# Weight sums in 32 spread pieces, and 512-column block products in the gated feed-forward

## The chip, the cores and the metric

One core of one Trainium2 chip runs the whole kernel. The metric is device time in microseconds (us), measured over the whole execution. The engines are named as the profile names them: PE (TensorE, the matrix multiplier), with PEld for its weight loads, DVE (VectorE), ACT (ScalarE), POOL (GpSimd) and SP (SyncE, which here only issues transfers). Sixteen DMA engines move data between HBM and on-chip memory, and also from HBM to HBM.

## The reference, cut to what matters

Two layers of an encoder work on 512 tokens of width 1024, all in float32. Each layer adds three things to the residual x: a mixer (neighbourhood attention, "NA", and grouped-query attention, "GQA", side by side), a cross attention to 256 memory tokens, and a gated feed-forward part with a short convolution. Only the last is computed differently by the change:

```python
def conv_ffn(h, w_up, conv_w, conv_b, w_down):
    u = h @ w_up                                   # 512 x 1024 times 1024 x 5632
    up = jnp.pad(u, ((0, 0), (1, 1), (0, 0)))
    u = up[:, :-2] * conv_w[0] + up[:, 1:-1] * conv_w[1] + up[:, 2:] * conv_w[2] + conv_b
    gate, val = jnp.split(u, 2, axis=-1)           # 2816 columns each
    return (jax.nn.silu(gate) * val) @ w_down
```

## The kernel before, in words

**Precision.** A matrix product in float32 is made of three reduced ones. Every operand is kept as a rounded part ("hi") and the rest ("lo"), and `mm3` (line 902) adds hi·hi, hi·lo and lo·hi in one PSUM bank. A weight tile is loaded by SP into one of three `raw` buffers, ACT rounds it to `hi` (line 784), POOL or DVE subtracts to get `lo` (line 785). Up to four such pairs exist; `get_w` prepares two tiles ahead of the one in use.

**Feed-forward units.** The 5632 columns of w_up are taken as 22 units j: 128 gate columns and the matching 128 value columns, for all 512 tokens. Units 0 to 5 (`PLAIN = 6`) are plain products: two sides, eight slices of the inner dimension, three matmuls of 512 token columns each, 48 in all. Units 6 to 21 use a block scheme with seven products in place of eight. Inner dimension, gate/value and token halves are each cut in two; with sums and differences of weight blocks and of token blocks, seven products of half the inner dimension and half the tokens (4 slices, three matmuls of 256 columns, so 84 matmuls) give both sides of the unit. `up_forms` (line 1922) does this in three PSUM banks, a, b and c, which it reads out with ACT copies and DVE additions between the products and after them. Then `convolve` applies the taps, the gate and the split of the result. From unit 6 on, rows of the down projection (six or five units times three matmuls of 512 columns for each of 8 rows and group) stand between the units.

**Weight sums.** The block scheme needs, for each layer, two matrices made out of w_up: `dr_sums` and `dr_diffs`, in HBM. `make_form` (line 704) makes one half of one of them in one call: a copy from HBM to HBM issued by ACT (the "base copy"), and then an accumulating transfer issued by POOL (line 714) on top of it. Each covers 16 units, 512 rows of 2048 columns, 4 MB. It is called in the first four steps of the neighbourhood attention of each layer (`na_quanta`, line 1683). One accumulating transfer reads another half, so it waits for that to be done.

**What sets the order.** The kernel is traced by loops that weave attention steps with filler products. SP issues its transfers in the order of this trace. For PE, ACT, DVE and POOL a planner (`Order`, line 348) reads the trace, gives each instruction a cost and a due time (the `Step.times` and `FAR_` numbers), and fixes an order by engine; there is no reordering when the kernel runs. An instruction that waits holds up everything behind it on its engine.

**Token operands.** Units 0 to 2 use unscaled tokens and multiply the PSUM result by the norm (`up_finish`). From unit 3 (`SCALED`) the tokens are scaled first (`scale_tokens`), split into hi and lo (`split_tokens`), and their block sums are made one by one (`token_forms`).

## Time and profile before

| | |
|---|---|
| median of 3 runs | 1416.34 us (1416.06 to 1418.67) |
| the profiled execution: its own time, and its span | 1416.2 us, 1414.3 us |
| PE busy | 1324.3 us, 94% of the span |
| DVE, ACT, POOL busy | 60%, 56%, 51% |
| mean granted TensorE clock | 0.969 of full |
| DMA | 229.78 MB, mean 162 GB/s |

The span runs from the first to the last instruction, and the execution's own time is 1.9 us longer. The stages of layer 0 lie at about 0 to 198 us (neighbourhood attention and its projections), 198 to 265 (grouped-query attention), 265 to 350 (memory attention) and 350 to 745 (feed-forward); layer 1 has the same stages at about 745 to 1400. In a table of windows each row gives, for a stretch, the busy time of each engine with its instruction count, the mean granted clock (PEclk, 1.00 is full), the busy share of the DMA engines and the rate in GB/s. Work of PE that is lost in a stretch is its idle time and, where the clock is below 1.00, that share of the busy time.

### The profile page before, as it was taken

How to read it: one execution, taken by the hardware profiler on the slowest of the kernel's cores; microseconds unless marked ns; L12 is line 12 of the kernel's file. 1: busy time of each engine (PE TensorE's matmuls, PEld its weight loads, DVE VectorE, ACT ScalarE, POOL GpSimd, SP SyncE). 2: the span in 40 equal slices, each digit the busy share in tenths (PEclk: the TensorE clock that was granted, in tenths of full speed). 3: DMA queues.
4: the chain of work that ended last, by engine and by line, in shares of the span. 5: the costliest groups of instructions: out<-in, count | busy, mean ns of one | idle time of the engine just before them, and what ended most of it. 6: DMA issues, size and time to landing. Idle time of an engine off the chain costs nothing.

```text
span 1414.3 us, 20974 instructions
## 1 busy us (share of the span) xinstructions
PE 1324.3 (94%) x7595; PEld 1158.5 (82%) x7595; DVE 843.6 (60%) x1729; ACT 788.1 (56%) x1459; POOL 721.3 (51%) x526
## 2 busy tenths in 40 slices
PE   9775899989999999999997759999899999999998
PEld 8664788868879999999886558888788899999997
DVE  6243787747596655555542538877576856554554
ACT  7244687646565555555542537875564555555544
POOL 2343696562645444444643337956453654444443
PEclk9887999999999999999998889999999999999999
DMA  7999958641324565555458998377322255555552
GB/s 237 307 305 247 222 142 179 141 134 42 113 85 127 147 171 145 149 144 150 120 163 296 325 262 201 107 178 161 107 68 82 86 168 149 162 150 145 150 154 75
DMA packets 262087, 229.78 MB, mean 162 GB/s; under 512 B 6880, under 2 KB 242912, under 8 KB 253792
## 3 DMA queue, kind: packets, MB, share of 16 engines
q1 hardware_dynamic: 253120, 160.94, 39.1%
q0 software_dynamic: 4224, 33.55, 11.6%
q10 hardware_dynamic: 4640, 33.95, 6.9%
q8 instruction: 60, 0.98, 0.3%
q14 instruction: 43, 0.35, 0.1%
HBM read 218.45 MB, written 69.21 MB: 203 GB/s over the span
## 4 chain that ended last, share of the span: by engine, by line
PE 78%; DMA 12%; DVE 3%; POOL 2%; ACT 2%; issue 1%; SPq 0%; POOLq 0%; ACTq 0%
PE mm L102 52%; PE sc L102 19%; PE tr L102 4%; DMA raw<-in_w_in 4%; DMA raw<-in_w_mem_q 3%; DMA t<-in_memT 2%; PE tr L1563 2%; POOL lo L785 1%; DMA dr_sums<-in_w_up 1%; DMA dr_diffs<-in_w_up 1%; DMA r<-in_bias 1%; PE tr L1408 1%; PE tr L1754 0%; ACT hi L784 0%; DVE t L1863 0%
## 5 line engine op out<-in xcount | busy, mean ns | idle before, releaser
L785 POOL TENSOR_TENSOR lo<-raw,hi 128x512 fp32r<-128x512 f32 (+3 forms) x293 | 521.4, 1789 | 538.3 <-ACT hi L784 486.7
L784 ACT CAST hi<-raw 128x512 fp32r<-128x512 f32 (+3 forms) x361 | 288.2, 812 | 269.3 <-DMA raw<-in_w_in 68.9
L102 PE MATMUL mm<-r,hi 128*128 128x512 f32 (+1 forms) x1344 | 387.5, 369 | 5.7 <-DVE xg L1008 5.7
L102 PE MATMUL mm<-xg,hi 128*128 128x512 f32 (+1 forms) x960 | 271.1, 368 | 3.2 <-ACT xg L1006 2.2
L102 PEld LDWEIGHTS mm<-r,hi 128*128 128x128 f32 x1344 | 238.6, 190 | 41.5 <-DVE xg L1008 6.1
L102 PE MATMUL mm<-r,lo 128*128 128x512 f32 (+1 forms) x704 | 251.3, 359 | 0.0
L102 PEld LDWEIGHTS mm<-xg,hi 128*128 128x128 f32 x960 | 173.0, 192 | 32.0 <-ACT xg L1006 2.6
L102 PE MATMUL mm<-xg,lo 128*128 128x512 f32 (+1 forms) x480 | 175.4, 365 | 0.0
L102 PE MATMUL sc<-r,hi 128*128 128x256 f32 (+1 forms) x832 | 163.9, 292 | 0.0
L102 PEld LDWEIGHTS mm<-r,lo 128*128 128x128 f32 x704 | 133.2, 189 | 20.2
L102 PEld LDWEIGHTS sc<-r,hi 128*128 128x128 f32 x832 | 133.7, 191 | 4.8
L102 PE MATMUL mm<-hi,xg 128*128 128x512 f32 (+1 forms) x384 | 117.9, 378 | 19.1 <-ACT t L1467 16.0
L102 PE MATMUL sc<-r,lo 128*128 128x256 f32 (+1 forms) x416 | 121.3, 291 | 0.0
L102 PEld LDWEIGHTS mm<-xg,lo 128*128 128x128 f32 x480 | 92.0, 192 | 14.6
L102 PEld LDWEIGHTS mm<-hi,xg 128*128 128x128 f32 x384 | 72.3, 201 | 30.2 <-ACT t L1467 16.3
L102 PE MATMUL sc<-r,r 128*128 128x256 f32 (+1 forms) x352 | 76.7, 340 | 18.4 <-ACT t L1386 18.4
L1063 POOL TENSOR_SCALAR t<-t,s 128x512 f32<-128x512 f32 (+1 forms) x112 | 67.0, 618 | 45.7 <-DVE s L1547 26.8
L102 PEld LDWEIGHTS sc<-r,lo 128*128 128x128 f32 x416 | 79.6, 191 | 1.2
L1950 DVE TENSOR_TENSOR tr<-mm,t 128x256 f32<-128x256 f32 x32 | 13.9, 433 | 111.5 <-PE mm L102 111.5
L785 DVE TENSOR_TENSOR lo<-raw,hi 128x1024 fp32r<-128x1024 f32 (+1 forms) x68 | 66.5, 978 | 20.2 <-ACT hi L784 20.1
L102 PEld LDWEIGHTS sc<-r,r 128*128 128x128 f32 x352 | 55.0, 197 | 25.7 <-ACT t L1386 19.8
L1863 DVE SCALAR_TENSOR_TENSOR t<-sc,minus,t 128x504 f32<-128x504 f32 (+1 forms) x128 | 56.1, 478 | 31.4 <-ACT t L1856 30.7
(210 smaller groups left out, 2296.1 us busy)
## 6 DMA issues: line engine op xcount, KB each, us to landing
raw<-in_w_up SPq DMA_DIRECT2D x56, 512.0 KB, 3.8
dr_sums<-in_w_up ACTq DMA_DIRECT2D x4, 4096.0 KB, 24.0
dr_diffs<-in_w_up ACTq DMA_DIRECT2D x4, 4096.0 KB, 19.3
raw<-dr_sums SPq DMA_DIRECT2D x32, 512.0 KB, 4.6
raw<-dr_diffs SPq DMA_DIRECT2D x32, 512.0 KB, 3.9
raw<-in_w_in SPq DMA_DIRECT2D x25, 512.0 KB, 5.4
raw<-in_w_down SPq DMA_DIRECT2D x32, 384.0 KB, 3.4
dr_sums<-in_w_up POOLq DMA_DIRECT2D x2, 4096.0 KB, 26.8
```

What stands on the lines that cost most here:

```text
L102: return self.engine.matmul(out, lhsT, rhs, **k)
L784: act.copy(hi[:, k], raw[:, k])
L785: (POOL if eng[0] == "P" else DVE).tensor_sub(lo[:, k], raw[:, k], f(hi)[:, k])
L1063: eng.tensor_scalar(e, e, sums[:, col : col + 1], 1.0, op0=ALU.mult, op1=ALU.mult)
L1408: PE.transpose(tr[:, (2 * i + c) * P : (2 * i + c + 1) * P], es[j][:, i, c * P : (c + 1) * P], ident)
L1563: PE.transpose(tr[:, k * P : (k + 1) * P], es[j][:, k * P : (k + 1) * P], ident)
L1863: DVE.scalar_tensor_tensor(cc[:, dst], u[:, src], wi, cc[:, dst], op0=ALU.mult, op1=ALU.add)
L1950: DVE.tensor_add(b[:, halves[1]], second, u2)
```

## The change

- `PLAIN` becomes 4: units 4 and 5 are block products too. `SCALED` is gone: units 0 to 3 all use unscaled tokens.
- The weight sums are made for four groups of units, (4, 4), (8, 4), (12, 5), (17, 5) as first unit and count. With two layers and four halves each that is 32 pieces, each a base copy of 512 rows by 512 or 640 columns (1 or 1.25 MB) and an accumulating transfer of the same size. The base copy is now issued by SP.
- The pieces wait in a list. One is taken at every third step of the grouped-query attention (six a layer), at four steps of the memory attention, and at every even unit of the feed-forward, in this order until the list is empty: layer 0 takes 10 before its feed-forward and 11 in it, and five of those already belong to layer 1.
- A token block holds its rounded part and the rest side by side, 256 columns each. A product is now, for each slice, one matmul of 512 columns (rounded weights times both) and one of 256 (the weights' rest times the rounded tokens): 56 matmuls a unit in place of 84. Since hi·hi and hi·lo then stand in two halves of a bank, each readout adds the halves: seven ACT copies, seven DVE and three POOL additions of 256 columns a unit, where there were three ACT copies and three DVE additions.
- All three blocks of tokens are split after unit 1, the sums are made after unit 2 and split after unit 3.
- The planner counts POOL's transfers as far (16 us, 1.3 us of POOL), and the base copies as ordinary ones.

The core of the diff (the new names are explained above; what is left out renames and moves):

```diff
-PLAIN = 6
-SCALED = 3
+PLAIN = 4
+SHARES_OF_FORMS = [(4, 4), (8, 4), (12, 5), (17, 5)]
...
-FAR_NS, FAR_POOL = 45000.0, 1500.0
+FAR_NS, FAR_POOL = 16000.0, 1300.0
...
+    form_queue = [(l, g, n) for l in range(DEPTH) for g in range(len(SHARES_OF_FORMS)) for n in range(4)]
...
+        l, g, n = form_queue.pop(0)
+        j, nj = SHARES_OF_FORMS[g]
...
-        act.dma_start(dst, base)
-        nc.gpsimd.dma_start(dst, more, accum_op=ALU.add, max_dma_last_dim=4 * 2048)
+        SP.dma_start(dst, base)
+        nc.gpsimd.dma_start(dst, more, accum_op=ALU.add, max_dma_last_dim=4 * P * nj)
...
         def na_quanta(s):
-            if s < 4:
-                make_form(l, s, ACT_IN_ORDER)
...
+        def gqa_quanta(s):
+            if s % 3 == 0:
+                make_form()
+            return [GQA_SLOT[s]]
...
+        def mem_quanta(s):
+            if s in (0, 2, 4, 6):
+                make_form()
+            return [MEM_FILL[s]]
...
+        def token_blocks():
             for name, k, n in (("b11", 0, 0), ("b21", 1, 0), ("b22", 1, 1)):
-                xform[name] = [v[:, 4 * k : 4 * k + 4, halves[n]] for v in (ffn.hi, ffn.lo)]
+                xform[name] = [rtile((2, S)) for _ in range(2)]
+                for v, src in zip(xform[name], quarter(k, n)):
+                    ACT.copy(v[:, :, halves[0]], src)
+                    DVE.tensor_sub(v[:, :, halves[1]], src, f(v)[:, :, halves[0]])
...
         def up_forms(j):
-            a, b, c = ps_s(), ps_t(), ps_mm()
+            a, b, c = ps_mm(), ps_t(), ps_s()
...
-                    mm3(ps, wh[:, i], wl[:, i], hi[:, k], lo[:, k], start and k == 0, k == 3, skip_group_check=not start)
+                    both = xform[form][k // 2][:, k % 2]
+                    PE.matmul(bank, wh[:, i], both, start=start and k == 0, stop=False, skip_group_check=True)
+                    PE.matmul(bank[:, halves[0]], wl[:, i], both[:, halves[0]], start=False, stop=k == 3, skip_group_check=True)
...
+            product(a, "gate", 0, "b11")
+            ACT.copy(p1, al)
+            DVE.tensor_add(p1, ah, p1)
+            product(b, "gate", 1, "b21")
+            ACT.copy(gb, bl)
+            POOL.tensor_add(gb, gb, p1)
+            DVE.tensor_add(bh, bh, gb)
+            product(c, "sums", 0, "t1")
+            ACT.copy(p5, cl)
+            DVE.tensor_add(p5, ch, p5)
+            product(a, "sums", 1, "t2", False)
+            ACT.copy(u2, al)
+            DVE.tensor_add(u2, ah, u2)
+            product(c, "diffs", 0, "b22", False)
+            ACT.copy(vc, cl)
+            POOL.tensor_add(vc, vc, u2)
+            DVE.tensor_add(bl, ch, vc)
+            product(a, "diffs", 1, "t3", False)
+            ACT.copy(va, al)
+            POOL.tensor_add(va, va, p5)
+            DVE.tensor_add(cl, ah, va)
+            product(a, "val", 0, "t4", False)
+            ACT.copy(l4, al)
+            DVE.tensor_add(ch, ah, l4)
+            convolve(j, [b, c])
...
+            if n % 2 == 0:
+                make_form()
             if n == 0:
                 up_first()
                 scale_tokens()
+                token_blocks()
             elif n > 1:
                 up(n)
+                if n == PLAIN - 2:
+                    token_sums()
+                elif n == PLAIN - 1:
+                    split_sums()
```

The planner and the loops move instructions, which the diff does not show. Three moves follow; in a row stand the line of the kernel, the operation, the tile written, the tiles read and the shape (partitions by columns); "x2" is two such instructions in a row.

First, the base copies. ACT in the neighbourhood attention of layer 0, before: `dr_sums` is one matrix of weight sums, `hi` rounded weights.

```order
L784 CAST hi_393<-raw_312 128x512 x2
L1059 ACTIVATE r_401<-mm_405,s_328 128x4x64 x2
L79 DMA dr_sums_78<-in_w_up 512x2048
L784 CAST hi_520<-raw_391 128x512 x2
L784 CAST hi_591<-raw_399 128x512
L1059 ACTIVATE r_402<-mm_458,s_328 128x4x64
L784 CAST hi_591<-raw_399 128x512
L79 DMA dr_sums_78<-in_w_up 512x2048
L1059 ACTIVATE r_402<-mm_458,s_328 128x4x64
```

Two base copies of 4 MB stand among its work; with the change ACT issues none. SP in the grouped-query attention of layer 0, with the change (`raw` are loads of weights):

```order
L79 DMA raw_1700<-in_w_out 128x4x256
L79 DMA dr_sums_78<-in_w_up 512x512
L79 DMA raw_1777<-in_w_out 128x4x256
L79 DMA raw_1842<-in_w_mem_kv 128x8x128
L79 DMA dr_sums_78<-in_w_up 512x512
L79 DMA raw_1899<-in_w_mem_kv 128x8x128
L79 DMA raw_2001<-in_w_out 64x4x256 x2
L79 DMA dr_diffs_79<-in_w_up 512x512
```

Base copies now stand between the weight loads of SP's own queue, one to every one to three loads. Second, SP in the feed-forward of layer 0, with the change (`in_w_up 128x4x128` are the value weights of a unit):

```order
L79 DMA raw_4390<-dr_sums_80 128x8x128
L79 DMA raw_4418<-dr_diffs_81 128x8x128
L79 DMA raw_4452<-in_w_up 128x4x128
L79 DMA dr_diffs_85<-in_w_up 512x640
L79 DMA raw_4486<-in_w_down 128x6x128
L79 DMA raw_4513<-in_w_up 128x8x128
```

Where the load of the down weights (`in_w_down`) came straight after that of the value weights, a base copy of 1.25 MB now goes ahead of it. Third, ACT in a block unit, before (`t<-sc` and `t<-mm` are the readouts, L1856 and L1865 the convolution and the gate):

```order
L1942 COPY t_4710<-sc_4707 128x256
L1056 CAST r_4678<-tr_4546 128x512
L784 CAST hi_4776<-raw_4716 128x768
L1946 COPY t_4711<-mm_4709 128x256
L1948 COPY t_4710<-sc_4707 128x256
L784 CAST hi_4808<-raw_4748 128x1024
L1856 ACTIVATE t_4826<-tr_4708,par 128x512
L784 CAST hi_4844<-raw_4780 128x1024
```

and with the change (L1961 to L1982 are the readouts, L789 the rounding of weights, L1870 the convolution, L1879 the gate):

```order
L1961 COPY t_4625<-mm_4622 128x256
L1968 COPY t_4626<-sc_4624 128x256
L1964 COPY t_4625<-tr_4623 128x256
L1879 ACTIVATE tr_4476<-t_4579 128x512
L789 CAST hi_4710<-raw_4660 128x1024
L1971 COPY t_4627<-mm_4622 128x256
L1062 CAST r_4593<-tr_4476 128x512
L1974 COPY t_4627<-sc_4624 128x256
L789 CAST hi_4744<-raw_4686 128x1024
```

Seven copies of banks stand where three stood, and the roundings of weights, each of which waits for a load, stand between them.

104 lines of the change are left out of this document (40 added, 64 removed).

## The prediction

> **What bounds the kernel now.** I first read the engines' shares at the head of the page (the span, 1414.3 us, stands in the table above), and then a table of windows, stage by stage.
>
> ```profile
> PE 1324.3 (94%) x7595; PEld 1158.5 (82%) x7595; DVE 843.6 (60%) x1729; ACT 788.1 (56%) x1459; POOL 721.3 (51%) x526
> ```
>
> ```profile
> core 0: us, PE busy (x) PEld busy (x) DVE busy (x) ACT busy (x) POOL busy (x), PEclk, DMA share, GB/s
> 50.00:125.00 75.00, 42.74 (x177) 33.72 (x176) 20.66 (x56) 26.53 (x70) 23.64 (x27) 0.77 0.95 304
> 125.00:175.00 50.00, 46.06 (x244) 38.74 (x244) 33.07 (x95) 32.39 (x86) 30.67 (x35) 0.93 0.94 220
> 175.00:275.00 100.00, 99.79 (x525) 82.92 (x525) 79.62 (x166) 74.00 (x159) 74.32 (x75) 1.00 0.62 150
> 275.00:300.00 25.00, 19.33 (x82) 15.63 (x81) 14.51 (x24) 12.09 (x20) 13.62 (x8) 0.93 0.79 185
> ...
> 425.00:675.00 250.00, 250.00 (x1728) 233.85 (x1727) 141.07 (x266) 135.93 (x200) 119.59 (x58) 1.00 0.52 147
> 750.00:800.00 50.00, 29.65 (x127) 24.01 (x126) 14.44 (x40) 16.83 (x45) 11.18 (x13) 0.80 0.97 314
> ...
> 825.00:875.00 50.00, 35.04 (x186) 29.78 (x184) 28.20 (x72) 23.87 (x61) 24.13 (x29) 0.83 0.97 228
> 875.00:975.00 100.00, 99.94 (x530) 83.27 (x529) 81.30 (x169) 77.04 (x162) 75.44 (x77) 1.00 0.59 144
> 975.00:1025.00 50.00, 45.99 (x222) 37.93 (x222) 29.44 (x63) 26.01 (x52) 26.61 (x16) 0.97 0.55 141
> ```
>
> Two regimes show. From 425 to 675 (and from 175 to 275, and 875 to 975) PE is busy all the time at full clock: PE is the bound, and only fewer or shorter matmuls help. In the other rows PE loses time while the DMA engines are busy at 0.8 to 0.97. Lost work is idle time plus the clock's share of the busy time. 50 to 125: 32.3 + 0.23 x 42.7 = 42.1. 125 to 175: 3.9 + 3.2 = 7.2. 750 to 800: 20.4 + 5.9 = 26.3. 825 to 875: 15.0 + 6.0 = 20.9. These four, all in neighbourhood attention, are **96.5 us**. The entries to the memory attention, 275 to 300 (5.7 + 1.4) and 975 to 1025 (4.0 + 1.4), add **12.4 us**.
>
> Who fills the DMA engines there? The chain of waits, the timeline of the issuing queues and the waits of SP:
>
> ```profile
> 40.02 25.89 DMA raw<-in_w_in
> 86.62 30.87 DMA t<-in_memT
> ...
> 269.50 20.65 DMA raw<-in_w_mem_q
> ...
> 822.37 21.90 DMA raw<-in_w_in
> ```
>
> ```profile
> 38.10 0.59 ACTq L79 DMA_DIRECT2D dr_sums<-in_w_up  x1
> 91.40 0.50 ACTq L79 DMA_DIRECT2D dr_diffs<-in_w_up  x1
> ```
>
> ```profile
> 264.27 1.03 POOL L714 DMA_DIRECT2D dr_diffs<-dr_sums  x1
> ```
>
> ```profile
> SPq L79 <- DMA dr_sums<-in_w_up: 52.3, 4, 13.6
> ```
>
> Ordinary loads of 0.25 to 0.5 MB take 16 to 31 us in the stretches in which the 4 MB base copies (first issue 38.1, last 91.4) and the last accumulating transfer (264.3) run. SP even stands 52 us behind base copies before it may issue its next load. So the lost 109 us are paid for the weight sums.
>
> **The change, part by part.**
>
> *Block products on PE.* Merged rows of the chain in the feed-forward, and from 400 to 436:
>
> ```profile
> 405.89 30.17 PE mm L102 x132
> 437.50 1.44 PE tr L102 x12
> ...
> 451.69 1.44 PE tr L102 x12
> ```
>
> A 512-column matmul takes 30.17 / 132 = 0.2286 us, a 256-column one 1.44 / 12 = 0.120. A block unit had 84 x 0.120 = 10.08 us and gets 28 x (0.2286 + 0.120) = 9.76, so 0.32 less; 16 units and two layers give 10.2. Units 4 and 5 had 48 x 0.2286 = 10.97 and get 9.76; four such units give 4.8. Together **-15.0 us**, straight on the bound. The rest of a unit's period (451.69 - 437.50 = 14.19) is 18 down matmuls, unchanged.
>
> The Trainium skill ("TensorE: Matmul & The Clock Gate", section "Back-to-back issue gap") speaks against most of this: it gives a warm gap of N/2.4 + 2.5 ns, 109 and 216 ns here, by which (an estimate) a unit would go only from 9.17 to 9.10 us and the sum would be 7.4 in place of 15.0. The rows above, with 120 and 229 ns, disagree with it; they decide.
>
> *Base copies out of the neighbourhood attention.* Nothing of the weight sums is left in it; of the 22.8 MB moved from 50 to 125 (75 x 304) most were the four base copies of 4.2 MB. Bounds: all 96.5 comes back, or, if other loads take the place, nothing. The row nearest to the state after is 175 to 275: the same attention loop at a DMA share of 0.62, with an accumulating transfer in it (rows of 214 to 240 below), loses 0.2 of 100. I take 85%, **-82 us**; the rest stays for bias and memory loads and for SP's copies within the chip, which are all in this stage.
>
> *Where the transfers go.* Part 3 of the page prices them:
>
> ```profile
> q0 software_dynamic: 4224, 33.55, 11.6%
> q10 hardware_dynamic: 4640, 33.95, 6.9%
> ```
>
> (0.116 + 0.069) x 1414.3 = 262 us of all 16 engines, so 8.2 for each of the 32 new pieces if smaller rows cost no more: 3.1 base copy, 5.1 accumulation. Six come in the 67 us of grouped-query attention, which without its accumulation needs some 16 us of DMA: 65 of 67, almost full. What a load suffers beside an accumulation, and what a unit can bear, by the transfers' issue to landing from 214 to 240 and from 440 to 700, and by rows of the timeline on the gate weights of one unit (and one more subtraction, on DVE):
>
> ```profile
> dr_sums<-dr_sums POOLq DMA_DIRECT2D x1, 4096.0 KB, 25.9
> raw<-in_w_mem_kv SPq DMA_DIRECT2D x2, 512.0 KB, 11.5
> ```
>
> ```profile
> raw<-in_w_up SPq DMA_DIRECT2D x14, 512.0 KB, 4.4
> ```
>
> ```profile
> 479.44 0.37 SPq L79 DMA_DIRECT2D raw<-in_w_up  x1
> 484.72 1.05 ACT L784 CAST hi<-raw 128x1024 fp32r<-128x1024 f32 x1
> 485.85 2.41 POOL L785 TENSOR_TENSOR lo<-raw,hi 128x1024 fp32r<-128x1024 f32 x1 [1.60 <-ACT hi L784]
> 488.46 1.21 DVE L785 TENSOR_TENSOR lo<-raw,hi 128x1024 fp32r<-128x1024 f32 x1
> 492.70 0.40 PE L102 MATMUL sc<-xg,hi 128*128 128x256 f32 x2
> ```
>
> 11.5 us were borne in grouped-query attention without loss, since weights are loaded long ahead: 0 for its 12 pieces. In the feed-forward a load is rounded 484.72 - 479.44 = 5.3 us after its issue and lands after 4.4, so it may be 0.9 late; then ACT, in order, stands, and behind the rounding stand its readouts of PSUM, on which the next products wait. A base copy ahead delays a load by up to 3.1 us, an accumulation beside it by up to 5.1. Bounds per piece: 0 (both fall between loads, or the weights' lead on PE covers it: 492.70 less 485.85 + 2.41 is 4.4 us) and 5.1 - 0.9 = 4.2. The planner knows the base copies, so I take 1.0 for the 12 pieces there: **+12** (0 to 50). For the memory attention's eight pieces 0.5 each, **+4** (0 to 14, by the 12.4 us that 8 MB cost at its entries). Of these 12.4 I expect half back, since smaller accumulations of the last steps still run there: **-6** (0 to -12.4). POOL's 32 issues of 1.03 us are 16 a layer, between work that fills half of it: 0.
>
> *Readouts.* A unit gains four ACT copies, four DVE additions and three POOL additions:
>
> ```profile
> 483.01 0.37 ACT L1946 COPY t<-mm 128x256 f32<-128x256 f32 x1 [0.68 <-PE mm L102]
> 485.95 0.43 DVE L1950 TENSOR_TENSOR tr<-mm,t 128x256 f32<-128x256 f32 x1 [3.51 <-PE mm L102]
> ```
>
> ```profile
> 143.22 0.72 POOL L1473 TENSOR_TENSOR t<-t,t 128x256 f32<-128x256 f32 x1
> ```
>
> ACT +1.5, DVE +1.7, POOL +2.2 us. From 425 to 675 a unit of 14.19 us holds 7.7, 8.0 and 6.8 of them; now 9.2, 9.7 and 9.0 of about 13.87, up to 70%. From 175 to 275 they are at 74 to 80% with PE full, so the amount is covered. The order is tighter: the second product in bank c comes one product (28 / 7 = 4 slices, 1.39 us) after the first, and in between ACT must copy and DVE add, 0.68 to start, 0.37 and 0.43, 1.48 with nothing in the way. The same holds between the second and third product in bank a. Down rows or the next unit's products fill such gaps where the planner can. Units 4 and 5 have no down rows. I take 0.2 for each of 36 units, **+7** (0 to 40).
>
> Splitting tokens earlier moves the same work; its cover is units 1 to 3, about 33 us of PE, and DVE is the engine that could be late: **+1** (0 to 6).
>
> **Sum**, against the profiled execution's own 1416.2 (span 1414.3, 1.9 around it; the median is 1416.34, so nothing is to be converted): 1416.2 - 15.0 - 82 - 6 + 12 + 4 + 7 + 1 = 1337.2. Forecast **1337 us**.
>
> **Rivals.**
>
> *All hidden.* The pieces and readouts cost nothing and 95% of the stalls go: 1416.2 - 15.0 - 92 - 12 = 1297, about 1300. For it: PE loses nothing from 175 to 275 under a full DMA. Against: the 0.9 us of slack.
>
> *The transfers find a new bound in the feed-forward and memory attention.* Each piece costs what the slack does not hold: 12 x 4.2 = 50 and 14, the entries give nothing back: 1416.2 - 15.0 - 82 + 50 + 14 + 8 = 1391. For it: just-in-time loads. Against: a piece comes only with every second unit. Beside it stands the Trainium skill ("DMA: Bandwidth & Descriptors", section "Queues, rings and completion order"): an engine takes one queue's descriptors in ring order and alternates between queues packet by packet. By that rule a base copy in SP's queue delays every load behind it fully, while the accumulation only takes its turn, with shorter rows than before; no run here shows SP's queue with such a copy in it.
>
> *Slower: readouts become the chain.* Each block unit waits at three places (c again, a twice) for a copy and an addition behind a rounding of 1.05 or a subtraction of 1.21 us (rows above), up to 1.3 us more than the 0.1 above, and nothing fills it: 36 x 3 x 1.4 = 151. Without its readout term the forecast is 1330, 86 under the time before, so it decides from 86 / 36 = 2.4 us a unit on; at 151 the time is 1481. Against: before, the planner kept PE full with the same banks.
>
> **How the numbers follow.** Forecast 0.53, all hidden 0.22, new DMA bound 0.20, readout chain 0.05. The forecast's own range is 1315 to 1360. The range of 8 in 10 takes in most of the hidden case and the lower part of the DMA bound: 1300 to 1378. About 0.2% is what a measurement here tells from no change; faster by more than that 0.94, the same 0.01, slower 0.05.
>
> **What would show it.** In the profile after: no wait of PE over 10 us in 50 to 125 and after layer 1 begins, PEclk 1.00 there; 28 matmuls of 512 and 28 of 256 columns a unit at a period of 13.87; ACT's roundings waiting for `raw` loads in the feed-forward of layer 0 only, a few us in all, against none in layer 1. Wrong would be: weights of the mixer still landing after 15 us (the base copies were not the cause); periods of layer 1's units well over 14 (readouts); layer 0's feed-forward over 20 us longer than layer 1's (pieces).

## The result, and the profile after

The changed kernel takes **1407.67 us** (median of 6 runs, 1402.57 to 1412.40); the kernel before, run beside it, 1419.28 us (1416.06 to 1421.14). The ratio is 0.9924, with a 95% interval of 0.9897 to 0.9951: faster, clear of the scatter of the runs, but by 0.8% where the prediction had 5.6%. The profiled execution took 1408.72 us, with a span of 1406.9 us.

The head of the page after, and a table of windows (the columns are those of the table in the prediction):

```profile
PE 1325.9 (94%) x6731; PEld 1110.0 (79%) x6731; DVE 932.4 (66%) x1901; ACT 826.6 (59%) x1627; POOL 840.1 (60%) x658
...
50.00:125.00 75.00, 74.52 (x413) 63.47 (x413) 53.39 (x147) 52.71 (x140) 49.03 (x55) 1.00 0.51 151
175.00:275.00 100.00, 94.04 (x478) 79.04 (x476) 65.79 (x134) 59.99 (x121) 62.74 (x54) 0.97 0.76 191
350.00:425.00 75.00, 62.57 (x287) 50.63 (x286) 57.48 (x98) 40.52 (x72) 40.60 (x27) 0.89 0.63 157
425.00:675.00 250.00, 224.03 (x1098) 185.35 (x1096) 145.12 (x278) 127.22 (x226) 141.87 (x96) 0.96 0.73 193
875.00:925.00 50.00, 44.68 (x229) 37.46 (x227) 32.02 (x71) 31.32 (x69) 30.48 (x34) 0.93 1.04 256
1050.00:1100.00 50.00, 43.92 (x193) 35.10 (x192) 48.22 (x78) 28.84 (x51) 27.85 (x17) 0.90 0.31 87
1100.00:1375.00 275.00, 260.26 (x1327) 216.28 (x1326) 176.19 (x343) 151.43 (x271) 162.55 (x106) 1.00 0.50 144
```

Lost work (idle time and the clock's share of the busy time) shows where the gain went. From 50 to 125 only 0.5 us is lost, where it was 42.1: the stalls of the neighbourhood attention are gone whole, and so are those at the memory attention. But 175 to 275 now loses 8.8 and 875 to 925 8.4, the grouped-query attentions; and the feed-forwards, which lost next to nothing before (0.6 from 350 to 425, nothing from 425 to 675), lose 19.3 (350 to 425), 34.9 (425 to 675), 10.5 (1050 to 1100) and 14.7 (1100 to 1375). That is 97 of the some 112 us that the gain is short (1408 against 1416 less the 109 of the stalls and the some 11 that the new products should save, below); the rest lies in stretches not shown and in the clock column, which is rounded to a hundredth.

In the grouped-query attention POOL stands at an accumulation whose base copy has not landed, and a transpose on PE waits for POOL's work behind it (waits from 175 to 200; the columns are us in total, times, longest):

```profile
POOL dr_sums L719 <- DMA dr_sums<-in_w_up: 9.8, 1, 9.8
...
PE tr L1569 <- POOL t L1069: 6.0, 1, 6.0
```

In the block units the chain of waits repeats unit by unit. One period in layer 1 (start, us, what), and PE's row at its end:

```profile
1181.93 1.29 PE mm L102 x7
...
1183.25 0.63 ACT hi L789
...
1183.90 0.03 DVE lo L790
...
1184.51 0.43 DVE sc L1983
1184.93 0.81 DVE t L1877 x2
...
1185.76 1.39 DVE t L1877 x2
1187.15 0.34 DVE t L1962
...
1187.54 1.68 PE mm L102 x8
1189.22 1.41 PE sc L102 x8
...
1197.75 1.29 PE mm L102 x7
```

```profile
1187.54 0.50 PE L102 MATMUL mm<-xg,hi 128*128 128x512 f32 x1 [1.22 <-DVE t L1962]
```

The period is 1197.75 - 1181.93 = 15.8 us, where 13.87 was expected. The last product of a unit ends at 1183.22 and frees a pair of weight buffers; ACT rounds the next weights into it (0.63), DVE subtracts (`lo`), and behind that, in DVE's fixed order, come the unit's last readout (L1983), three large convolution parts (L1877; of the four instructions in its two rows one has only 7 columns) and only then the readout of the *next* unit's first product (L1962), for which the second product in bank a waits. The chain takes 4.3 us from 1183.22 to 1187.54; PE's work beside it ends 1.22 us earlier. Two of the prediction's signs of being wrong have thus come: the period of layer 1's units is well over 14 us, and layer 0's feed-forward loses 54.2 us (19.3 + 34.9) where layer 1's loses 25.2 (10.5 + 14.7).

### The profile page after: what moved, and what is told of

It is laid out like the page before. It is cut to its first block, busy times and chain, and to the rows that moved or that the text cites. A ratio compares the mean times of both kernels' runs of the same rounds, so it can differ in the third digit from the quotient of the medians.

```text
span 1406.9 us, 19861 instructions
## 1 busy us (share of the span) xinstructions
PE 1325.9 (94%) x6731; PEld 1110.0 (79%) x6731; DVE 932.4 (66%) x1901; ACT 826.6 (59%) x1627; POOL 840.1 (60%) x658
## 4 chain that ended last, share of the span: by engine, by line
PE 45%; DVE 4%; DMA 2%; ACT 2%; issue 1%; POOL 1%; POOLq 0%; SPq 0%; ACTq 0%; DVEq 0%
PE mm L102 35%; PE sc L102 6%; DVE t L1877 2%; PE tr L102 2%; DMA dr_sums<-in_w_up 2%; POOL lo L790 1%; PE tr L1569 1%; ACT hi L789 1%; PE tr L1414 1%; DVE r L1908 0%; DVE r L1899 0%; ACT t L1870 0%; DVE r L1923 0%; PE tr L1763 0%; DVE t L1962 0%
## 5 line engine op out<-in xcount | busy, mean ns | idle before, releaser
L789 ACT CAST hi<-raw 128x512 fp32r<-128x512 f32 (+3 forms) x369 | 294.3, 813 | 308.5 <-PE mm L102 174.7
L102 PE MATMUL mm<-xg,hi 128*128 128x512 f32 x1008 | 347.4, 404 | 37.6 <-DVE t L1962 29.5
L102 PE MATMUL mm<-xg,lo 128*128 128x256 f32 (+1 forms) x720 | 237.4, 330 | 0.0
L790 DVE TENSOR_TENSOR lo<-raw,hi 128x1024 fp32r<-128x1024 f32 (+1 forms) x76 | 92.3, 1214 | 96.0 <-ACT hi L789 93.5
L102 PEld LDWEIGHTS mm<-xg,lo 128*128 128x128 f32 x720 | 140.1, 195 | 14.6
L102 PE MATMUL sc<-r,hi 128*128 128x512 f32 x208 | 78.9, 419 | 6.2 <-DVE t L1969 3.8
L102 PE MATMUL sc<-xg,hi 128*128 128x512 f32 x208 | 74.8, 407 | 1.1 <-DVE xg L1936 1.0
L1877 DVE SCALAR_TENSOR_TENSOR t<-sc,minus,t 128x504 f32<-128x504 f32 (+1 forms) x144 | 66.5, 473 | 5.1 <-ACT t L1870 5.1
L1063 DVE TENSOR_TENSOR r<-tr,r 128x512 fp32r<-128x512 f32 x84 | 57.0, 687 | 18.0 <-ACT r L1062 13.3
L102 PE MATMUL mm<-lo,xg 128*128 128x512 f32 (+1 forms) x192 | 68.5, 357 | 0.0
L1877 DVE SCALAR_TENSOR_TENSOR t<-tr,par,t 128x504 f32<-128x504 f32 (+1 forms) x144 | 65.9, 476 | 2.6 <-ACT t L1870 1.7
L1992 DVE TENSOR_TENSOR xT<-xT,mm 128x512 f32<-128x512 f32 x48 | 32.7, 682 | 47.1 <-PE mm L102 47.1
## 6 DMA issues: line engine op xcount, KB each, us to landing
dr_sums<-in_w_up SPq DMA_DIRECT2D x8, 1280.0 KB, 10.2
```

What stands on the lines that cost most here:

```text
L102: return self.engine.matmul(out, lhsT, rhs, **k)
L789: act.copy(hi[:, k], raw[:, k])
L790: (POOL if eng[0] == "P" else DVE).tensor_sub(lo[:, k], raw[:, k], f(hi)[:, k])
L1063: DVE.tensor_sub(lo, ps, f(hi))
L1877: DVE.scalar_tensor_tensor(cc[:, dst], u[:, src], wi, cc[:, dst], op0=ALU.mult, op1=ALU.add)
L1992: DVE.tensor_add(xT[m], xT[m], pm)
```

## The experiments

The kernel before, run beside each group, took 1420.1 to 1421.5 us; differences of two or three microseconds between groups are not read. "Old products" are those of the kernel before (three matmuls of 256 columns), "new products" those of the change.

| run | what it is | us | ratio to before (95%) |
|---|---|---|---|
| old_spread | old products, spread pieces | 1370.9 | 0.9648 (0.9621 to 0.9674) |
| new_big | new products, large transfers | 1507.7 | 1.0607 (1.0579 to 1.0635) |
| new_nosums | new products, no sums made | 1370.6 | 0.9642 (0.9621 to 0.9664) |
| old_nosums | old products, no sums made | 1310.8 | 0.9222 (0.9202 to 0.9242) |
| new_nosums_plain6 | and units 4, 5 plain | 1312.2 | 0.9235 (0.9203 to 0.9267) |
| new_nosums_bank | and a second bank | 1335.4 | 0.9399 (0.9358 to 0.9440) |
| new_nosums_copies | and less work on DVE | 1362.5 | 0.9596 (0.9577 to 0.9615) |
| old_late | accumulations a slot later | 1363.4 | 0.9615 (0.9575 to 0.9655) |
| old_attention | and all in attention | 1358.0 | 0.9558 (0.9536 to 0.9579) |
| after_plain6 | the change, units 4, 5 plain | 1405.2 | 0.9901 (0.9884 to 0.9918) |
| old_paced | both transfers held by POOL | 1343.3 | 0.9464 (0.9448 to 0.9480) |
| old_even | single transfers, even | 1358.2 | 0.9561 (0.9547 to 0.9575) |
| new_even6 | the same, new products | 1352.7 | 0.9520 (0.9504 to 0.9536) |
| new_even4 | the same, units 4, 5 as blocks | 1440.0 | 1.0134 (1.0112 to 1.0156) |
| old_ahead | all ahead of the block units | 1319.3 | 0.9290 (0.9275 to 0.9305) |
| new_ahead6 | the same, new products | **1315.1** | 0.9265 (0.9249 to 0.9281) |

### Each half alone, and neither with sums

The first kernel takes the pieces without the products, the second the products without the pieces. The last two make no sums; units load columns of w_up of the same size in their place:

```diff
-            cols(("sums", j), made[l][g][0], 0, KC, P * (j - j0), P, "D")
-            cols(("diffs", j), made[l][g][1], 0, KC, P * (j - j0), P)
+            cols(("sums", j), t["w_up"][l], 0, KC, P * j, P, "D")
+            cols(("diffs", j), t["w_up"][l], 0, KC, D_FF + P * j, P)
...
-                make_form()
+                pass
```

> One half of the change alone: the products, readouts and token splits of the kernel before (units 6 to 21 as blocks, three matmuls of 256 columns), but the weight sums in spread pieces (three groups of units, 24 pieces of 1.25 to 1.5 MB, same places). Theory A (three costs, each too small in the prediction, ate the gain: pieces about 39 us, readouts about 40, the move to block products and the earlier token splitting about 25): only the pieces' cost is left, so 1419 - 109 + 39 = about 1350 us. Rival B (the pieces ate nearly all of it, readouts and token splits cost next to nothing): only the 15 us of the block products are missing against the changed kernel, about 1408 + 15 = 1423 us. Rival C (the readouts and token splits ate all of it, pieces cost next to nothing): 1419 - 109 = about 1310 us.

> The other half alone: block products of 512 columns, new readouts, units 4 and 5 as blocks, but the weight sums in four large transfers a layer in the neighbourhood attention as before (rows of 2304 columns, base copies on ACT's queue, accumulations in rows of 1152). Theory A: the stalls of the neighbourhood attention come back (109 us), the pieces' 39 go, readouts and transition stay: 1408 + 109 - 39 = about 1478 us, slower than before. Rival B: 1419 - 15 = about 1404. Rival C: about 1408 + 109 = 1517.

> The changed kernel with no weight sums made: units 4 to 21 load columns of the same size straight from w_up in the place of sums and differences. It leaves the making of the sums out, so that the outputs are not the reference's; every other instruction stays. It prices all pieces at once. Theory A: 1408 - 39 = about 1369 us, layer 0's feed-forward no longer than layer 1's, the period of layer 1's units still near 15.8. Rival B: about 1310. Rival C: about 1405.

> The kernel before with no weight sums made, in the same way (the outputs are not the reference's). Its attention stalls should go whole: 1419 - 109 = about 1310 us in every theory. The difference to the changed kernel without sums is the price of the new products, readouts and token splits with no transfer in it: Theory A +59 (1369 - 1310), Rival B -15 to 0, Rival C +95, and the prediction on record had it at -15 + 7 + 1 = -7.

Measured: 1370.9, 1507.7, 1370.6 and 1310.8 us. The stalls were worth what the prediction said: without sums the old kernel is 111 us shorter, where the prediction had put 109 down to them. **The new products cost 60 us with no transfer in the way**, where the prediction had them 7 us to the good. The pieces cost 60 us with the old products and 37 with the new. So theory A is right for the 1311 and 1371, 20 too low for old_spread and 30 too low for new_big. B fails in all but the 1311, on which all agree, and C fails for old_spread and new_nosums (its 1517 is the nearest to new_big). Why the large transfers cost 137 us beside the new products (1507.7 - 1370.6) and 111 beside the old ones stays open; they now cover 18 units a layer in place of 16, and the accumulations go in rows of 1152 columns in place of 2048. Windows of the old products without sums, and then of the new:

```profile
375.00:650.00 275.00, 274.09 (x1838) 253.69 (x1838) 154.24 (x286) 150.13 (x226) 135.44 (x69) 1.00 0.51 146
```

```profile
325.00:400.00 75.00, 63.19 (x289) 51.31 (x287) 65.91 (x114) 41.18 (x70) 34.05 (x21) 0.93 0.29 83
400.00:650.00 250.00, 235.81 (x1212) 196.79 (x1211) 160.30 (x309) 139.86 (x250) 152.63 (x99) 1.00 0.52 146
1000.00:1075.00 75.00, 66.57 (x305) 54.48 (x304) 66.15 (x116) 41.91 (x72) 37.81 (x23) 0.93 0.34 96
1075.00:1350.00 275.00, 260.08 (x1330) 216.74 (x1329) 172.36 (x336) 147.94 (x266) 161.37 (x103) 0.99 0.48 137
```

The loss has two places in both layers: the entry into the block units (16.2 and 13.1 us) and the block units themselves (14.2 and 17.5).

### What is in the 60 us

Three kernels without sums. Units 4 and 5 plain again:

```diff
-PLAIN = 4
-SHARES_OF_FORMS = [(4, 4), (8, 4), (12, 5), (17, 5)]
+PLAIN = 6
+SHARES_OF_FORMS = [(6, 6), (12, 5), (17, 5)]
```

> The changed kernel without sums (1371 us; the outputs are not the reference's), with units 4 and 5 plain again: block sums of tokens are made after unit 4 and split after unit 5. Theory A: the loss at the start of the feed-forward (11.9 + 3.8 us from 350 to 400, and 11.4 from 1025 to 1050) comes from the tokens' sums being due after only four plain units and goes; 16 block units with the new readouts stay: 1371 - 28 + 5 = about 1348 us. Rival F (the loss comes from the first block unit itself, whenever it comes, or from splitting the blocks after unit 1): about 1372 to 1376 us.

The later products of bank a in a bank d, so that the second no longer waits for the first one's readout (three readouts then lack the first product):

```diff
-            product(a, "sums", 1, "t2", False)
-            ACT.copy(u2, al)
-            DVE.tensor_add(u2, ah, u2)
+            product(d, "sums", 1, "t2")
+            ACT.copy(u2, dl)
+            DVE.tensor_add(u2, dh, u2)
```

> The changed kernel without sums, with the later products of bank a in a bank of their own, so that the second product of that bank no longer waits until ACT and DVE have read out the first (the first product's result is then missing from three readouts; the outputs are not the reference's, the count of instructions is the same). Theory G (that one wait is the readouts' price, 29.5 + 37.5 us at PE and its loads in layer 1's feed-forward): the period of layer 1's units falls from about 15.6 to 14.1, some 18 us a layer: about 1335 us. Rival H (behind it stand the next handovers, c again and a third and fourth time, with nearly the same delay): 1360 to 1371 us.

Copies in place of the tokens' subtractions (the rest parts of blocks and sums are then wrong):

```diff
-                    DVE.tensor_sub(v[:, :, halves[1]], src, f(v)[:, :, halves[0]])
+                    ACT.copy(v[:, :, halves[1]], src)
```

> The changed kernel without sums (1371 us), and the rest parts of the token blocks and token sums are plain copies on ACT in place of subtractions on DVE (outputs are not the reference's; the later units' order on VectorE is as in the 1371 us kernel). It takes about 14 us of DVE's work away from the stretch at 325 to 375, where DVE is busy 24.8 and 21.2 of 25 us, and adds about 8 to ACT. Theory A2 (DVE's amount of work there is the bound, 13 to 17 us a layer): 28 less at most: 1343 to 1350 us. Rival M (the first block units themselves or their weights are late there): 1365 to 1371 us.

Measured: **1312.2** us with six plain units (58 of the 60 gone, more than either theory), **1335.4** with the second bank (theory G's value; its two runs took 1332.3 and 1338.6, so that the price is 32 to 38 us and the exact hit is luck), 1362.5 with copies (8 gone of an expected 21 to 28, and below M's 1365 to 1371 too: neither theory holds alone). Six plain units:

```profile
325.00:400.00 75.00, 73.20 (x341) 60.44 (x340) 70.51 (x114) 41.72 (x66) 38.69 (x21) 1.00 0.33 95
400.00:650.00 250.00, 250.00 (x1280) 211.94 (x1281) 165.78 (x328) 154.07 (x269) 163.85 (x110) 1.00 0.53 153
```

The same readouts now cost nothing from 400 to 650, with DVE busier (165.78 us against 160.30). Not the number of readouts but their place makes the difference. DVE's rows between a unit's last readout (L1983) and the next unit's first (L1962), first with four plain units and then with six:

```profile
1143.46 0.69 DVE L790 TENSOR_TENSOR lo<-raw,hi 128x512 fp32r<-128x512 f32 x1 [2.89 <-ACT hi L789]
1144.07 0.43 DVE L1983 TENSOR_TENSOR sc<-mm,t 128x256 f32<-128x256 f32 x1
1144.42 1.65 DVE L1877 SCALAR_TENSOR_TENSOR t<-tr,par,t 128x504 f32<-128x504 f32 x3
1145.98 0.73 DVE L1877 SCALAR_TENSOR_TENSOR t<-sc,minus,t 128x504 f32<-128x504 f32 x1
1146.63 0.41 DVE L1962 TENSOR_TENSOR t<-mm,t 128x256 f32<-128x256 f32 x1
```

```profile
1123.11 0.43 DVE L1983 TENSOR_TENSOR sc<-mm,t 128x256 f32<-128x256 f32 x1 [2.40 <-ACT t L1982]
1123.79 0.74 DVE L1877 SCALAR_TENSOR_TENSOR t<-tr,par,t 128x504 f32<-128x504 f32 x1 [0.25 <-ACT t L1870]
1124.45 0.68 DVE L790 TENSOR_TENSOR lo<-raw,hi 128x512 fp32r<-128x512 f32 x1
1125.05 0.22 DVE L1877 SCALAR_TENSOR_TENSOR t<-tr,par,t 128x7 f32<-128x7 f32 x1
1125.24 0.42 DVE L1962 TENSOR_TENSOR t<-mm,t 128x256 f32<-128x256 f32 x1
```

With four, the subtraction of new weights stands ahead of the last readout, and three large convolution parts ahead of L1962 (of the three instructions in the row of 1.65 us one has 7 columns); with six, the subtraction stands behind the last readout, and one large part is ahead of L1962. No run set the order by itself: both came from the planner, for different numbers of plain units. The second bank takes the wait away and leaves the order, and the block units lose 0.5 of 250 us:

```profile
400.00:650.00 250.00, 249.47 (x1286) 211.11 (x1286) 166.89 (x331) 153.21 (x268) 161.63 (x105) 1.00 0.53 151
```

Together these two show the wait at bank a's second product to be the price of the readouts. (The profile is of the run of 1338.6; it loses 8 us from 775 to 825, in layer 1's attention, where one DVE instruction at L1112 takes 6.9 us; why is open.)

The entry is another matter: the second bank leaves most of its 16.2 and 13.1 us, 11.4 from 325 to 400 (75 - 0.98 x 64.91) and 11.2 from 1000 to 1075. With copies, layer 0 loses 3.9 us from 325 to 375 (12.4 without them: 50 - 0.93 x 40.42), as DVE's amount of work would have it:

```profile
325.00:375.00 50.00, 46.10 (x217) 36.58 (x216) 42.87 (x83) 38.93 (x70) 22.54 (x14) 1.00 0.35 100
```

In layer 1 the total stayed (12.9 us from 1000 to 1075) but its place moved: from 1000 to 1050 the loss fell from 11.3 to 6.8, and from 1050 to 1075 it rose from 1.8 to 6.3, where the chain is the loop of the block units again (L1983, six pieces of L1877, L1962). The kernel with the second bank, in which that loop cannot hold PE, tells the two apart. Its row for layer 1's entry:

```profile
1000.00:1075.00 75.00, 65.07 (x312) 51.91 (x311) 64.11 (x108) 44.03 (x76) 39.07 (x25) 0.98 0.38 105
```

Its chain there is DVE's work, but for gaps of half a microsecond at most, from 999.5 to 1035.7, most of it the tokens' scaling, blocks and sums (L1899 to L1939) and convolution parts. So in both layers the entry's loss goes with the work on DVE, shown by taking work away in layer 0 and by the chain in layer 1.

### When a piece is issued, and by whom

All three have old products. First, the accumulation one slot after its base copy; then also all 12 pieces of a layer in its attention stages; then both transfers on POOL's queue, held to their place in its order, with two pieces at units 0 and 3 of the feed-forward. The core of the last edit, against old_spread:

```diff
-        SP.dma_start(dst, base)
-        nc.gpsimd.dma_start(dst, more, accum_op=ALU.add, max_dma_last_dim=4 * P * nj)
+            POOL_IN_ORDER.dma_start(dst, base)
+            form_pending.append((dst, more, 4 * P * nj))
+        if then:
+            dst, more, row = then
+            POOL_IN_ORDER.dma_start(dst, more, accum_op=ALU.add, max_dma_last_dim=row)
```

> The old products with spread pieces (1371 us), and each accumulation issued by POOL one slot after its base copy was issued by SP (at the next step that takes a piece), in place of at once. Theory D (in the pieces' stretches the loss is POOL standing in its fixed order at an accumulation whose base copy has not landed, with weight subtractions and attention work behind it: 23.1 + 4.1 us from 175 to 235 and 27 us in layer 0's feed-forward): the 25 us of the grouped-query attention go nearly whole and about half of the 23 in the feed-forward: about 1335 us, no wait of POOL over 2 us for a base copy. Rival E (the DMA engines, busy at 0.96 to 1.0 from 175 to 300, are the cause, and ordinary loads are late whatever POOL does): 1365 to 1375 us, POOL's waits gone but PE waiting for loads in their place.

> As the run with late accumulations, and all 12 pieces of a layer stand in its own attention stages: five in the later steps of the neighbourhood attention, three in the grouped-query, four in the memory attention, none in a feed-forward (the kernel before without sums keeps the DMA engines busy only 0.22 to 0.4 from 100 to 400, against 0.5 to 0.57 in the feed-forward). Theory D: the rest of the feed-forward's loss goes too: 1315 to 1325 us, near the 1311 with no sums at all. Rival E: the same transfers in fewer microseconds cost at least as much as in the first spread kernel: 1350 to 1375 us.

> Old products; both transfers of a piece issued by POOL and held to their place in its order (in the earlier runs SP ran ahead of the work and issued five base copies within 33 us, from 142 to 175, and one of its issues took 17.6 us); the accumulation one slot after its base copy; 12 pieces a layer at steps 3, 5, 7 of the neighbourhood attention, 2, 7, 12 of the grouped-query, 0, 2, 4, 6 of the memory attention and at units 0 and 3. Theory L (bunching and the wait behind SP's queue are what the pieces still cost, 47 us in the kernel with all pieces in attention): 1320 to 1335 us, no stretch of 25 us with over 4 us lost. Rival E (the amount of transfer costs this much wherever it is put): 1350 to 1365 us.

Measured: 1363.4, 1358.0 and 1343.3 us. Theory D fell: a slot later gained 7.5 us, not 36, and old_attention lies in rival E's range (1350 to 1375) and not in D's. SP's issues in old_late (timeline from 140 to 180), and POOL's wait from 172 to 225:

```profile
142.27 0.56 SPq L80 DMA_DIRECT2D dr_sums<-in_w_up  x1
...
166.53 5.04 SPq L80 DMA_DIRECT2D dr_diffs<-in_w_up  x1
...
175.04 17.59 SPq L80 DMA_DIRECT2D dr_sums<-in_w_up  x1
```

```profile
POOL dr_sums L712 <- DMA dr_sums<-in_w_up: 22.3, 2, 21.8
```

SP runs ahead of the work as far as its load buffers let it, so five pieces that stand at spread places in the program start within 33 us (at 142.27, 156.02, 163.71, 166.53 and 175.04); the last one's issue alone takes 17.6 us, and POOL still waits 21.8 us for it. Held by POOL's order the same stretch loses nothing, with the DMA engines busier. Windows of old_late, then of old_paced:

```profile
175.00:225.00 50.00, 30.45 (x158) 25.44 (x157) 22.15 (x50) 20.69 (x45) 20.86 (x25) 0.80 0.93 221
```

```profile
175.00:225.00 50.00, 50.00 (x272) 42.17 (x271) 37.69 (x83) 35.09 (x76) 32.88 (x36) 1.00 1.00 254
```

So it is not the amount of transfer (rival E) that stalls this stretch. The time is 15 us below old_attention, whose places are near but not the same. It lies between the two ranges, 8 us above L's 1320 to 1335. What is left stands mainly ahead of the memory attention (11.9 us lost from 275 to 350, behind five transfers that leave POOL from 259.7 to 266.9) and at the start of the feed-forward (7.5 from 375 to 425).

### The same undoing in the changed kernel

after_plain6 is the changed kernel with `PLAIN = 6` and three groups of sums.

> The changed kernel with one number undone: units 4 and 5 plain again (three groups of sums, 24 pieces, at the same places; new products and readouts for 16 units). Without sums this change was worth 58 us (1371 to 1312). In the fixed order of VectorE, counted from the kernels' own instruction lists, three convolution parts stand between the last readout of a unit and the first of the next in nearly all units of the changed kernel, and one in the 1312 us kernel; here it is three again in layer 1 and one to three in layer 0. Theory I (that order decides what the readouts cost; the rest of the 58 is the tokens' work, which six plain units cover): the 28 us of the start of the feed-forward go, the readouts' loss stays in layer 1 at about 15 us: 1408 - 28 + 5 = about 1385 us. Rival J (with six plain units the readouts are free in any order): the same as the old products with spread pieces, about 1372 us. Rival K (with the pieces in it, PE waits elsewhere anyway): about 1400 to 1408.

Measured: 1405.2 us. That is rival K's range; theory I is missed by 20, though the parts it names hold. Three windows:

```profile
175.00:225.00 50.00, 30.21 (x153) 25.12 (x152) 20.80 (x48) 20.67 (x45) 19.34 (x23) 0.80 0.92 219
400.00:675.00 275.00, 241.05 (x1176) 199.15 (x1175) 167.75 (x303) 137.26 (x243) 154.47 (x104) 0.95 0.78 200
1050.00:1250.00 200.00, 190.58 (x948) 158.16 (x947) 144.42 (x273) 112.69 (x194) 117.63 (x70) 1.00 0.46 129
```

The entries no longer lose, and layer 1's units lose 9.4 us from 1050 to 1250, with no transfer of the sums there. That is the price of an order with three convolution parts: PE waits 1.20 to 1.21 us for L1962 ahead of 1136.13, 1151.55 and 1166.90, as with four plain units. So the readouts' price goes with the order and not with the number of plain units. But the pieces, now 1.25 to 1.5 MB in place of 1 to 1.25, lose 25.8 us at the start of the grouped-query attention (8.8 in the changed kernel) and layer 0's feed-forward 46.0, where the old products with the same 11 pieces lose 23 (275 - 0.99 x 254.26). In old_spread, from 400 to 675:

```profile
400.00:675.00 275.00, 254.26 (x1719) 233.36 (x1718) 151.04 (x263) 130.25 (x199) 126.76 (x63) 0.99 0.82 215
```

So here pieces and readouts cost more together than the pieces alone; how much of it is the order, and how much the size of the pieces, no run separates.

### Evenly paced, and ahead of the block units

Each base copy and each accumulation now has a place of its own on POOL's queue, 24 places a layer. The three "even" kernels have 11 of them at units 0 to 10, the two "ahead" kernels only four at units 0 to 3:

```diff
-            if s in (4, 9, 14):
+            if s in (2, 5, 8, 11, 14):
...
-            if s in (0, 3, 6):
+            if s in (0, 1, 2, 3, 4, 5, 6, 7):
...
-            if n in (0, 1, 2, 3, 4, 5, 6, 7, 8, 9, 10):
+            if n in (0, 1, 2, 3):
```

> Old products with pieces spaced evenly: each base copy and each accumulation stands alone at its own place in POOL's order, 24 places a layer (seven steps of the neighbourhood attention, three of the grouped-query, three of the memory attention, units 0 to 10), an accumulation never at the place of a base copy. In the kernel before this (1343 us) four to six transfers still started within 28 us ahead of the memory attention, a load of w_up then took 17.7 us, and 33 us over the 1311 us without sums were left. Theory L (bunches are what is left): 1318 to 1330 us. Rival E (amount): 1340 to 1350 us.

> The same evenly spaced pieces with the new 512-column products and readouts for units 6 to 21 (six plain units). Its order on VectorE has one convolution part between the last readout of a unit and the first of the next in 12 of the first 14 such places and none to one in layer 1's first seven, as the 1312 us kernel without sums, where the kernel of 1405 us had three. Theory I (the order of VectorE decides the readouts' price, and pieces in the feed-forward make it worse only where they delay weights): within 10 us of the old products with the same pieces, 1320 to 1335 us. Rival N (new readouts and pieces cannot stand each other wherever they are: 57 us lost in layer 0's feed-forward at 1405 us against 23 with old products): 30 us or more above the old products, 1350 to 1370 us.

> The changed kernel (units 4 and 5 as blocks, order with three convolution parts in most units) with the same evenly spaced pieces (three groups of 8, 5 and 5 units). What the pieces took is mostly gone, what units 4 and 5 and the order take stays: the 58 us that separate 1371 and 1312 us without sums: Theory A/I: 50 to 60 us above the run with six plain units and the same pieces, about 1380 us. Rival O (the changed kernel's loss is mainly its pieces' places): within 20 us of it, 1335 to 1350 us.

> Old products with evenly paced pieces as in the kernel of 1358 us, but 20 of a layer's 24 transfers stand in the attention stages and the last four at units 0 to 3, so that none is under way once the block units run. In the 1358 us kernel the stretch from 100 to 375, with 13 transfers in it, lost nothing, and 375 to 475, with seven, lost 19 us, 2.7 each; layer 1 the same. Theory P (a transfer costs only where weights are loaded just in time, which is in the block units): 1315 to 1325 us, near the 1311 without sums. Rival E (more transfers in the attention stages bring their stalls back, as 47 us in the kernel whose pieces SP issued there): 1340 to 1358 us.

> The same places with the new 512-column products and readouts for units 6 to 21, six plain units (the order on VectorE has mostly one convolution part ahead of a unit's first readout, as in the 1312 us kernel). Theory P with I: within 10 us of the old products with the same places, 1315 to 1330 us. Rival E: 1340 to 1360.

Measured: 1358.2, 1352.7 and 1440.0; 1319.3 and **1315.1** us. Theory L fell (old_even is 15 us worse than old_paced, and above rival E's range too), and its trace gave theory P, whose ranges hold both "ahead" kernels. new_even6 is 5.5 us below old_even, as theory I had it, but both are later than its range. Windows of old_even, then of old_ahead.

```profile
100.00:375.00 275.00, 274.20 (x1387) 228.83 (x1386) 210.73 (x437) 184.22 (x365) 185.80 (x156) 1.00 0.56 154
375.00:475.00 100.00, 86.84 (x551) 80.52 (x550) 46.84 (x88) 44.09 (x65) 42.87 (x24) 0.91 0.84 211
```

```profile
100.00:375.00 275.00, 274.42 (x1392) 230.00 (x1391) 208.86 (x437) 184.19 (x366) 192.28 (x161) 1.00 0.68 183
375.00:475.00 100.00, 99.79 (x704) 93.78 (x703) 59.43 (x110) 55.68 (x83) 46.13 (x22) 1.00 0.62 165
```

In old_even 13 transfers from 100 to 375 cost 0.8 us and seven from 375 to 475 cost 21 (100 - 0.91 x 86.84). Moved ahead, they cost 0.6 and 0.2. Spacing was not even to the end: of the seven, two pairs left POOL within 0.7 us (at 377.2 and 377.9, 397.9 and 398.5). But old_ahead has such pairs too (two transfers each at 281.99 and 315.20) and loses nothing there. The weight sums then still take the DMA engines as long as ever; part 3 of new_ahead6's page (packets, MB, share of 16 engines):

```profile
q0 software_dynamic: 19200, 67.11, 20.7%
```

That is 0.207 x 1311.5 = 271 us of all 16 engines (262 before), for 3 us over new_nosums_plain6 and 8 with old products over old_nosums (both compare kernels of different groups). The same bytes in the same transfers cost 47 us in old_even. **At the same amount moved, a piece is priced by where it runs**, and, by old_late and old_paced, by who issues it and when. What the size of a single transfer does was not varied by itself. And with six plain units new products are level with old ones or a little better under the same transfers: 5 us with intervals apart, 4 us with intervals that overlap. With four (new_even4) they are 87 us slower than with six. Some 26 of these lie in the neighbourhood attentions, where its first group of eight units moves 2 MB a transfer (that the size is the cause is not shown); the other 60 agree with the 58 of the kernels without sums. The expected 1380 was missed by 60: by these 26, and because the kernels with six plain units came out some 30 above what it was added to.

new_ahead6 beats both kernels: 7.4% less than before, 6.6% less than the change.

## Why the prediction was wrong, step by step

| step | on record | what the runs show |
|---|---|---|
| block products on PE | -15.0 | about -11, by single rows |
| base copies out of neighbourhood attention | -82 of 96.5 | -95 |
| entries to memory attention | -6 of 12.4 | -12, all of it |
| pieces in the feed-forward | +12 | about +24, layer 0 only (54.2 lost from 350 to 675, 30.4 without sums) |
| pieces in the memory attention | +4 | 0 |
| pieces in the grouped-query attention | 0 | +17 |
| readouts | +7 (0 to 40) | about +35 |
| splitting tokens earlier | +1 (0 to 6) | about +29 |

The right column adds up to -13, and the profiled execution is 7.5 us shorter (1416.2 to 1408.7): some 6 us stay open.

The first half held: base copies and large accumulations were the cause of the stalls, and all of what they cost came back, in the rows named beforehand. (One reading was off and bore on nothing: of the losing rows, 975 to 1025 has a DMA share of 0.55 and not 0.8 to 0.97; its loss went too.) The range failed on the other half, in three terms.

*Splitting tokens earlier* is the step that failed outright. The prediction named the right engine ("DVE is the engine that could be late") and then took the cover from PE's 33 us without adding up DVE's own work there. The sum could have been made from the profile of before, where DVE was already that full late in the plain units (window from 400 to 425):

```profile
400.00:425.00 25.00, 24.88 (x110) 20.32 (x109) 22.47 (x41) 14.71 (x20) 12.14 (x6) 1.00 0.29 82
```

The change keeps the tokens' work and takes two plain units, 22 us of PE, away from over it; from 1000 to 1075 above DVE is busy 66.15 of 75 us and PE waits. 29 us (16.2 + 13.1) is the entry's loss without sums, and 23 of them stay with the second bank, so that up to 7 belong to the readouts. Taking work off DVE removed 8.5 of the 12.4 us from 325 to 375 in layer 0; in layer 1 the chain of the kernel with the second bank is DVE's work.

*Readouts* had the right mechanism ("between the second and third product in bank a"; a copy and an addition behind a rounding or a subtraction) but the wrong place and size. PE waits at the *second* product of bank a, which the prediction did not name; what stands ahead of the readout is not one rounding but the weight subtraction, the last unit's readout and its convolution, 4.3 us in all. About 35 us by the runs with a second bank (1371 to 1332 and 1339), 32 by the rows. Its bound of 0 to 40 held; the 0.2 us taken per unit was a guess between. The amount per unit was never the matter: with six plain units, and another order, the same readouts cost nothing.

*Pieces in the grouped-query attention* were set to 0 because a load had borne 11.5 us there. What failed was not a load but the pair: an accumulation waits on POOL for its base copy, and the attention's own work on POOL stands behind it. The prediction costed POOL's 32 issues at 1.03 us and did not ask what they wait for. *Pieces in the feed-forward* cost 2.2 us each (24 over 11) in place of 1.0, within the bounds, by the mechanism given: from 425 to 675 the roundings on ACT wait 14.2 us for loads of the sums and 10.2 for loads of the differences, and from 1100 to 1375, with no pieces, 1.2 and nothing.

For *block products* one product now takes 1.41 us (eight matmuls, row at 1189.22) against 1.44 before, so a unit gains 7 x 0.03 = 0.21 and not 0.32; 32 such units give 6.7, units 4 and 5 4.4. In whole kernels with such 32 units the new products are 5.5 us (old_even, new_even6) and 4.2 us (old_ahead, new_ahead6) better, readouts included. The Trainium skill's gap for a single warm matmul ("TensorE: Matmul & The Clock Gate", section "Back-to-back issue gap") gave the prediction an estimate of 7.4 (worked out again it is 7.3); the 11 lies between it and the 15.0.

Of the rivals, *all hidden* (1300) is what the design can do once units 4 and 5 are plain and the pieces stand ahead: 1315. The *new bound* (1391) came nearest in time, by luck: of its terms, the feed-forward's 50 measured 24, the memory attention's 14 nothing, and the entries gave all back. What brought the time there are the entry and the readouts, which it too put at 8 together. The *readout chain* did occur, at about 1 us a unit (35 over 36), below the 2.4 from which it would have decided. That +1 and +7 could each be 30 off at once was in no case's range; the upper end, 1378, let only one term fail at a time.

## What to carry to other kernels

Before work is moved ahead, add up the busy time of the engine that does it in the stretch that must now hold it, not the time of the engine that is to hide it. Where an order is fixed, a readout is priced by what stands ahead of it on its own engine; look for a loop that runs from a freed buffer through rounding and readout back to the next product, and compare its length with PE's work beside it. Background transfers were nearly free here where loads run far ahead and dear where loads are just in time: give them a queue that the loads do not use, hold them to a place in the order, and keep them out of just-in-time stages.

## What was not expected of the hardware

271 us of all 16 DMA engines beside a full PE cost 3 to 8 us, with a mean granted clock of 0.998 and 0.999 (old_ahead, new_ahead6).

An issue on SP can itself take long: 17.59 us at 175.04 above, with four base copies issued in the 33 us before it; an issue of the same kind took 0.56 at 142.27.

A subtraction of 512 columns on DVE takes 0.68 us alone and up to 2.9 beside a POOL subtraction. Rows of POOL and of DVE in new_nosums:

```profile
344.08 2.78 POOL L790 TENSOR_TENSOR lo<-raw,hi 128x1024 fp32r<-128x1024 f32 x1 [8.63 <-ACT hi L789]
```

```profile
344.51 2.90 DVE L1908 TENSOR_TENSOR r<-r,r 128x512 fp32r<-128x512 f32 x1
...
352.51 0.68 DVE L1908 TENSOR_TENSOR r<-r,r 128x512 fp32r<-128x512 f32 x1
```

DVE's 2.90 us end 0.55 after POOL's subtraction does. The Trainium skill ("SBUF — State Buffer", section "SBUF: two separate sides") states that DVE and GpSimd take a shared pair of ports exclusively, for a whole instruction, while the other one blocks; for DVE it names among others instructions with two inputs in SBUF, as here, beside a GpSimd instruction that reads SBUF. These rows agree. So DVE's busy time at the entry holds waiting too, and moving its work to POOL, which was not tried, would not give all of it back.
